# Seven row buffers instead of five, and a dense stage that gates each chunk at once with three activation tiles: one hybrid decoder layer on one Trainium2 core

## The chip, the cores and the metric

The kernel runs on one core of a Trainium2 chip. The metric is the device time of one execution in microseconds, the median of several runs; lower is better. Engines are named as the profile names them: PE (matrix engine), DVE (vector), ACT (scalar), POOL (GpSimd) and SP (the queue that issues most loads). The DMA engines move what SP, ACT and POOL issue.

## What is computed

One decoder layer for 1024 tokens of width 1024. An input projection feeds an mLSTM group of heads and an attention group of heads; both outputs are concatenated, projected and added to x. Then each token picks 128 single-neuron experts (8 heads, the best 16 of each) out of 16384, and adds what they give:

```python
def block(args):
    xb, ib, gb = args
    u = expert_u[ib]
    pre = jnp.einsum('td,tkd->tk', xb, u).astype(jnp.float32)
    a = jax.nn.gelu(pre, approximate=False) * gb
    return jnp.einsum('tk,tkd->td', a, expert_v[ib])
```

`ib` are a token's expert numbers and `gb` its gates (a softmax over the picked scores).

## The kernel before, in words

The 8 tiles of 128 tokens are cut into three groups: group 0 is tiles 0 and 1, group 1 tiles 2 to 5, group 2 tiles 6 and 7. Each group goes through a projection (`channels_in`, `project_*`), attention and mLSTM woven together (`attention`, `mlstm_half`), and `queries` (output projection, query projection, top-16 searches on DVE), then `pick`, which makes expert numbers and gates.

The experts are computed in two ways. Groups 0 and 2 are sparse: for each of a token's 128 experts, POOL gathers one row of 4 KB per token, 128 rows in one indirect DMA into a tile `gt` of 512 KB (`gather`, line 801), and DVE uses it in one instruction. `experts_in` (the U steps, line 813) multiplies and sums, `experts_out` (the V steps, line 854) multiplies and accumulates. For tile 0 the out step runs on PE instead (`experts_out_pe`, 64 steps with two gathers each, DVE line 835, PE line 842; called the W steps below). The order of the sparse work is fixed: U0 U1 W V1 U6 V6 U7 V7, where W is V0, with 128 gathers each.

Group 1 is dense. `spread_gates` writes a table of gates for all 16384 experts and its 512 tokens to DRAM (DVE line 722, ACT lines 726, 730 and 738, POOL line 732, 32 stores of 1 MB from line 739). `dense_experts` then runs over 16 expert groups of 8 chunks of 128 experts. A chunk's U part loads 512 KB (`ur`), splits it into a high and a low part on ACT and DVE (`uhi`, `ulo`), takes 24 matmuls of 512 columns into `pu`, and a Gelu on ACT (`da`, line 763). The gates of the expert group, 2 MB (`gg`, line 766), multiply `da` on DVE (line 769), the product is split (`dah`, `dal`), and the V part takes 24 matmuls a chunk into `pv`. That makes 6144 matmuls.

The program is written one part after another, but the order on each engine is made by a scheduler while the kernel is built. It moves an instruction past others as far as its inputs and the room in on-chip memory allow. Pools of tiles are stacked from two sides, and a pool opened where another lay must wait for the tiles there. The sparse pool that holds `gt` stays open from start to end, five tiles of 4 KB a partition; the pools of the dense stage are open only there. Each engine then runs its own list strictly in order.

Of the kernel before, what the change touches and what calls it, by code (L numbers as in the profile page):

```python
# [11 lines left out]
F32 = mybir.dt.float32  # L12
# [8 lines left out]
P = 128  # L21
T = 1024
D = 1024
# [7 lines left out]
EG = 8  # L31
TB = 16
# [11 lines left out]
def hybrid_layer(ctx, tc, x, g1, w_in, w_if, conv_w, conv_b, wq, wk, if_b, mh_g, skip, qn_g, kn_g,  # L44
                 rel_bias, onehot, w_out, g2, w_query, keys, expert_u, expert_ut, expert_v, out, dbg=None):
    nc = tc.nc
# [4 lines left out]
    sp = ctx.enter_context(tc.tile_pool(name="sparse", bufs=1))  # L51
# [12 lines left out]
    def pool(name, side="left"):  # L64
        return tc.tile_pool(name=name, bufs=1, side=side, reuse_waits="tile")
# [82 lines left out]
    def split(hi, lo, src):  # L148
        nc.scalar.copy(hi, src)
        nc.vector.tensor_tensor(lo, src, hi.bitcast(F32), op=ALU.subtract)  # L150

    def mm3(ps, lh, ll, rh, rl, first, last):
        nc.tensor.matmul(ps, lh, rh, start=first, stop=False)  # L153
        nc.tensor.matmul(ps, lh, rl, start=False, stop=False)  # L154
        nc.tensor.matmul(ps, ll, rh, start=False, stop=last)  # L155
# [552 lines left out]
    gate_d = dram.tile([GROUPS[DENSE][1] * P // TB, P, P * TB], F32, name="gate_d")  # L708
# [32 lines left out]
    def dense_experts(psu):  # L741

        tile0, TD = GROUPS[DENSE]
        DW = TD * P
        nb = DW // TB
        with pool("dh", "right") as dh, pool("du", "right") as du, pool("da", "right") as da, \
                pool("dl", "right") as dl, tc.tile_pool(name="psv", bufs=5, space=PS) as psv:
            th, tl = DENSE_IN
            acc = []
            for c0 in range(0, P, EG):  # L750
                ah, al, pre = [], [], []
                for c in range(c0, c0 + EG):
                    ur = du.tile([P, KD, P], F32, name="ur", bufs=2)
                    nc.sync.dma_start(ur, expert_ut[c])
                    uh = du.tile([P, KD, P], F32R, name="uhi", bufs=2)
                    nc.scalar.copy(uh, ur)  # L756
                    ul = du.tile([P, KD, P], F32R, name="ulo", bufs=2)
                    nc.vector.tensor_tensor(ul, ur, uh.bitcast(F32), op=ALU.subtract)  # L758
                    pp = psu.tile([P, DW], F32, name="pu")
                    for k in range(KD):  # L760
                        mm3(pp, uh[:, k], ul[:, k], th[:, k], tl[:, k], k == 0, k == KD - 1)
                    a = da.tile([P, DW], F32, name="da", bufs=EG + 1)
                    nc.scalar.activation(a, pp, AF.Gelu)  # L763
                    pre.append(a)
                gg = dl.tile([P, nb, EG, TB], F32, name="gg", bufs=1)
                nc.sync.dma_start(gg.rearrange("p b e t -> p b (e t)"),
                                  gate_d.rearrange("b p f -> p b f")[:, :, c0 * TB:(c0 + EG) * TB])
                for c, a in enumerate(pre, c0):
                    nc.vector.tensor_tensor(a.rearrange("p (b t) -> p b t", t=TB),
                                            a.rearrange("p (b t) -> p b t", t=TB), gg[:, :, c - c0], op=ALU.mult)  # L770
                    h = dh.tile([P, DW], F32R, name="dah", bufs=EG + 2)
                    l = dh.tile([P, DW], F32R, name="dal", bufs=EG + 2)
                    split(h, l, a)
                    ah.append(h)
                    al.append(l)
                if not acc:
                    for i in range(TD):
                        a = da.tile([P, D], F32, name="dacc", bufs=TD)
                        nc.sync.dma_start(a, x2_d[tile0 + i])
                        acc.append(a)  # L780
                for half in range(2):
                    cols = slice(half * 512, (half + 1) * 512)
                    po = [psv.tile([P, 512], F32, name="pv") for _ in range(TD)]
                    for c in range(c0, c0 + EG):
                        vr = dh.tile([P, 512], F32, name="vr", bufs=4)
                        nc.sync.dma_start(vr, expert_v.rearrange("(a c) d -> c a d", c=P)[c, :, cols])
                        vh = dh.tile([P, 512], F32R, name="vhi", bufs=2)
                        nc.scalar.copy(vh, vr)  # L788
                        vl = dh.tile([P, 512], F32R, name="vlo", bufs=2)
                        nc.vector.tensor_tensor(vl, vr, vh.bitcast(F32), op=ALU.subtract)  # L790
                        for i in range(TD):
                            s = slice(i * P, (i + 1) * P)
                            mm3(po[i], ah[c - c0][:, s], al[c - c0][:, s], vh, vl, c == c0, c == c0 + EG - 1)
                    for i in range(TD):
                        nc.vector.tensor_tensor(acc[i][:, cols], acc[i][:, cols], po[i], op=ALU.add)
            for i in range(TD):
                nc.sync.dma_start(out[(tile0 + i) * P:(tile0 + i + 1) * P], acc[i])

    def gather(table, idx, j):
        gt = sp.tile([P, D], F32, name="gt", bufs=5)  # L800
        nc.gpsimd.indirect_dma_start(out=gt, out_offset=None, in_=table,  # L801
                                     in_offset=bass.IndirectOffsetOnAxis(ap=idx[:, j:j + 1], axis=0))
        return gt
# [3 lines left out]
    def experts_in(t):  # L807
        h2 = sp.tile([P, D], F32, name="h2s", bufs=1)
        nc.sync.dma_start(h2, h2_d[t])
        pr = sp.tile([P, P], F32, name="pr_s", bufs=2)  # L810
        for j in range(P):
            gt = gather(expert_u, IDX[t], j)
            nc.vector.scalar_tensor_tensor(gt, gt, 1.0, h2, op0=ALU.mult, op1=ALU.mult,  # L813
                                           accum_out=pr[:, j:j + 1])
        a = sp.tile([P, P], F32, name="act", bufs=2)
        nc.scalar.activation(a, pr, AF.Gelu)
        nc.vector.tensor_tensor(a, a, GATE[t].rearrange("p h k -> p (h k)"), op=ALU.mult)
        COEF[t] = a
# [30 lines left out]
    def experts_out(t):  # L849
        acc = sp.tile([P, D], F32, name="acc", tag="acc", bufs=1)  # L850
        nc.sync.dma_start(acc, x2_d[t])
        for j in range(P):
            gt = gather(expert_v, IDX[t], j)
            nc.vector.scalar_tensor_tensor(acc, gt, COEF[t][:, j:j + 1], acc, op0=ALU.mult, op1=ALU.add)  # L854
        nc.sync.dma_start(out[t * P:(t + 1) * P], acc)
# [80 lines left out]
    for c in (psgx, pstx, psmx):  # L936
        c.__exit__(None, None, None)
    dense_experts(psu)
    psux.__exit__(None, None, None)
    ql.close()  # L940
    for step in "U0 U1 V0 V1 U6 V6 U7 V7".split():
        t = int(step[1])
# [81 lines left out]
```

## Time and profile before

| what | us |
|---|---|
| median of 3 runs (lowest, highest) | 3164.97 (3154.72, 3176.85) |
| the profiled execution's own time | 3162.73 |
| its span, from the first to the last instruction | 3160.9 |
| PE busy | 2763.9 |
| DVE busy | 2513.1 |
| POOL busy | 1439.0 |
| ACT busy | 1223.1 |

Times in views count from the span's start. The share of 16 DMA engines, the GB/s and the clock granted to PE are given by stretch; a clock of 1.0 is the upper of its two levels.

### The profile page before, as it was taken

What the parts mean: (1) busy time and instruction counts of PE and PEld (TensorE: products, weight loads), DVE (VectorE), ACT (ScalarE), POOL (GpSimd) and SP (SyncE); (2) the same over time, 40 slices, a digit from 0 to 9 for tenths busy, and PEclk for the clock granted to TensorE, in tenths of its full rate; (3) what the DMA queues carried; (4) which work ended last, traced back from release to release, by engine and by line L of the source; (5) the groups of instructions that cost most, each with busy time, mean ns of one, the idle gap of its engine ahead of it and who ended that gap; (6) DMA issues with size and microseconds to landing.
All of it is one profiled execution on the core that took longest, in us unless ns stands there. A gap on an engine that the chain in (4) does not pass through costs nothing.

```text
span 3160.9 us, 42101 instructions
## 1 busy us (share of the span) xinstructions
PE 2763.9 (87%) x13867; PEld 2180.5 (69%) x13867; DVE 2513.1 (80%) x5674; ACT 1223.1 (39%) x2265; POOL 1439.0 (46%) x1139
## 2 busy tenths in 40 slices
PE   6987766898679999776865999999999999999999
PEld 5877655676555554566753778787777888887787
DVE  4559986798854777899999888889887888988843
ACT  4643322454323223698972222233222332332222
POOL 0100665556643334465445555555554455555500
PEclk9979887797789999888986999999999999999999
DMA  6543899799987777688779999999999999999942
GB/s 195 180 157 112 300 312 359 277 321 325 318 278 253 247 263 258 192 298 297 261 241 329 346 325 336 335 331 329 324 326 325 319 339 344 326 326 340 321 144 74
DMA packets 370543, 891.45 MB, mean 282 GB/s; under 512 B 34023, under 2 KB 135399, under 8 KB 366228
## 3 DMA queue, kind: packets, MB, share of 16 engines
q0 software_dynamic: 147456, 536.94, 48.7%
q1 hardware_dynamic: 208724, 307.78, 29.4%
q10 hardware_dynamic: 14144, 44.05, 3.6%
q8 instruction: 109, 1.79, 0.2%
q14 instruction: 110, 0.90, 0.1%
HBM read 831.97 MB, written 61.38 MB: 283 GB/s over the span
## 4 chain that ended last, share of the span: by engine, by line
PE 38%; issue 17%; DVE 17%; DMA 15%; POOL 9%; ACT 3%; SPq 0%; POOLq 0%; DVEq 0%; ACTq 0%
POOL gt L801 9%; DMA gg<-gate_d 4%; PE accq L192 4%; DMA gt<-in_expert_u_dram,idx 4%; PE pu L154 3%; PE pv L154 3%; PE pu L155 3%; PE pu L153 3%; PE pv L155 3%; PE pv L153 3%; PE pov L842 3%; DVE gt L813 3%; DVE acc L854 2%; DMA gt<-in_expert_v_dram,idx 2%; PE acco L192 2%
## 5 line engine op out<-in xcount | busy, mean ns | idle before, releaser
L801 POOL DMA_INDIRECT gt<-in_expert_u_dram,idx x512 | 663.6, 1296 | 622.6 <-DVE gt L813 377.4
L801 POOL DMA_INDIRECT gt<-in_expert_v_dram,idx x384 | 502.3, 1308 | 432.5 <-DVE acc L854 320.0
L813 DVE SCALAR_TENSOR_TENSOR gt<-gt,h2s 128x1024 f32<-128x1024 f32 x512 | 617.5, 1218 | 64.3 <-DMA gt<-in_expert_u_dram,idx 63.3
L854 DVE SCALAR_TENSOR_TENSOR acc<-gt,act,acc 128x1024 f32<-128x1024 f32 x384 | 503.9, 1312 | 20.0 <-DMA gt<-in_expert_v_dram,idx 17.3
L153 PE MATMUL pu<-h2th,uhi 128*128 128x512 f32 x1024 | 409.4, 400 | 46.3 <-ACT da L763 27.9
L155 PE MATMUL pu<-h2th,ulo 128*128 128x512 f32 x1024 | 408.7, 399 | 10.8 <-DVE ulo L758 10.8
L154 PE MATMUL pv<-vlo,dah 128*128 128x512 f32 x1024 | 403.8, 394 | 9.6 <-DVE vlo L790 9.6
L154 PE MATMUL pu<-h2tl,uhi 128*128 128x512 f32 x1024 | 408.7, 399 | 0.0
L155 PE MATMUL pv<-vhi,dal 128*128 128x512 f32 x1024 | 401.6, 392 | 0.0
L788 ACT CAST vhi<-vr 128x512 fp32r<-128x512 f32 x256 | 157.4, 620 | 449.3 <-PE pv L155 428.0
L153 PE MATMUL pv<-vhi,dah 128*128 128x512 f32 x1024 | 319.6, 394 | 11.1 <-ACT vhi L788 7.4
L168 ACT CAST wh<-wr 128x512 fp32r<-128x512 f32 x291 | 178.5, 620 | 291.5 <-PE accq L192 64.5
L153 PEld LDWEIGHTS pu<-h2th,uhi 128*128 128x128 f32 x1024 | 194.9, 190 | 93.8 <-ACT da L763 29.1
L170 DVE TENSOR_TENSOR wl<-wr,wh 128x512 fp32r<-128x512 f32 x291 | 201.3, 700 | 71.6 <-ACT wh L168 70.5
L790 DVE TENSOR_TENSOR vlo<-vr,vhi 128x512 fp32r<-128x512 f32 x256 | 175.2, 685 | 92.2 <-ACT vhi L788 91.9
L756 ACT CAST uhi<-ur 128x1024 fp32r<-128x1024 f32 x128 | 134.4, 1051 | 271.8 <-PE pu L154 271.4
L801 POOL DMA_INDIRECT gt<-in_expert_v_dram,idxt x128 | 129.2, 1010 | 233.9 <-PE pov L842 204.3
L155 PEld LDWEIGHTS pu<-h2th,ulo 128*128 128x128 f32 x1024 | 194.5, 190 | 58.6 <-DVE ulo L758 12.2
L154 PEld LDWEIGHTS pv<-vlo,dah 128*128 128x128 f32 x1024 | 193.6, 189 | 56.9 <-DVE vlo L790 14.9
L153 PEld LDWEIGHTS pv<-vhi,dah 128*128 128x128 f32 x1024 | 192.4, 189 | 58.0 <-ACT vhi L788 11.3
L154 PEld LDWEIGHTS pu<-h2tl,uhi 128*128 128x128 f32 x1024 | 194.7, 190 | 46.3
L155 PEld LDWEIGHTS pv<-vhi,dal 128*128 128x128 f32 x1024 | 193.9, 189 | 41.9
(280 smaller groups left out, 5710.6 us busy)
## 6 DMA issues: line engine op xcount, KB each, us to landing
ur<-in_expert_ut_dram SPq DMA_DIRECT2D x128, 512.0 KB, 6.1
vr<-in_expert_v_dram SPq DMA_DIRECT2D x256, 256.0 KB, 5.6
wr<-in_w_in_dram SPq DMA_DIRECT2D x144, 256.0 KB, 4.8
gate_d<-gs ACTq DMA_DIRECT2D x32, 1024.0 KB, 6.7
gg<-gate_d SPq DMA_DIRECT2D x16, 2048.0 KB, 19.2
wr<-in_w_query_dram SPq DMA_DIRECT2D x96, 256.0 KB, 3.8
wr<-in_w_out_dram SPq DMA_DIRECT2D x48, 256.0 KB, 4.0
gt<-in_expert_u_dram,idx POOLq DMA_INDIRECT x512, 6.9
```

The lines of the kernel that those rows point to most:

```text
L153: nc.tensor.matmul(ps, lh, rh, start=first, stop=False)
L154: nc.tensor.matmul(ps, lh, rl, start=False, stop=False)
L155: nc.tensor.matmul(ps, ll, rh, start=False, stop=last)
L168: nc.scalar.copy(wh, wr)
L170: nc.vector.tensor_tensor(wl, wr, wh.bitcast(F32), op=ALU.subtract)
L192: nc.tensor.matmul(o, l, r, start=k == 0 and c == 0 and j == 0, stop=k == KD - 1 and j == 2, skip_group_check=True)
L756: nc.scalar.copy(uh, ur)
L788: nc.scalar.copy(vh, vr)
L790: nc.vector.tensor_tensor(vl, vr, vh.bitcast(F32), op=ALU.subtract)
L801: nc.gpsimd.indirect_dma_start(out=gt, out_offset=None, in_=table, in_offset=bass.IndirectOffsetOnAxis(ap=idx[:, j:j + 1], axis=0))
L813: nc.vector.scalar_tensor_tensor(gt, gt, 1.0, h2, op0=ALU.mult, op1=ALU.mult, accum_out=pr[:, j:j + 1])
L854: nc.vector.scalar_tensor_tensor(acc, gt, COEF[t][:, j:j + 1], acc, op0=ALU.mult, op1=ALU.add)
```

## The change

`gt` has seven buffers instead of five. In the dense stage the load of an expert group's gates stands ahead of the group's eight U parts instead of behind them; the gate product and its split follow each chunk's Gelu at once; and `da` has three buffers instead of nine (8 + 1). Nothing is computed differently. A `da` tile is 2 KB a partition, a `gt` tile 4 KB.

```diff
             for c0 in range(0, P, EG):
-                ah, al, pre = [], [], []
+                ah, al = [], []
+                gg = dl.tile([P, nb, EG, TB], F32, name="gg", bufs=1)
+                nc.sync.dma_start(gg.rearrange("p b e t -> p b (e t)"),
+                                  gate_d.rearrange("b p f -> p b f")[:, :, c0 * TB:(c0 + EG) * TB])
                 for c in range(c0, c0 + EG):
...
-                    a = da.tile([P, DW], F32, name="da", bufs=EG + 1)
+                    a = da.tile([P, DW], F32, name="da", bufs=3)
                     nc.scalar.activation(a, pp, AF.Gelu)
-                    pre.append(a)
-                gg = dl.tile([P, nb, EG, TB], F32, name="gg", bufs=1)
-                nc.sync.dma_start(gg.rearrange("p b e t -> p b (e t)"),
-                                  gate_d.rearrange("b p f -> p b f")[:, :, c0 * TB:(c0 + EG) * TB])
-                for c, a in enumerate(pre, c0):
                     nc.vector.tensor_tensor(a.rearrange("p (b t) -> p b t", t=TB),
                                             a.rearrange("p (b t) -> p b t", t=TB), gg[:, :, c - c0], op=ALU.mult)
...
-        gt = sp.tile([P, D], F32, name="gt", bufs=5)
+        gt = sp.tile([P, D], F32, name="gt", bufs=7)
```

The scheduler makes another order of it, well outside the lines of the diff. The lines of the changed kernel are up to three lower or higher than before (801 is 799, 813 is 811, 854 is 852, 769 is 767, 758 is 761, 790 is 788).

On POOL, before, in the second attention stretch: `idx` with expert_u are the U gathers, `rqo` is a step of a projection (here group 2's), `rmo` one of an mLSTM head (here group 1's).

```order
L161 TENSOR_TENSOR rqo<-rq,mhalf 128x8
L801 DMA gt<-in_expert_u_dram,idx 128x1024 x7
L161 TENSOR_TENSOR rqo<-rq,mhalf 128x8
L801 DMA gt<-in_expert_u_dram,idx 128x1024
L161 TENSOR_TENSOR rmo<-rm,mhalf 128x2
L801 DMA gt<-in_expert_u_dram,idx 128x1024 x6
L161 TENSOR_TENSOR rqo<-rq,mhalf 128x8
L801 DMA gt<-in_expert_u_dram,idx 128x1024 x12
L161 TENSOR_TENSOR rmo<-rm,mhalf 128x2
```

The same engine now, from the last mLSTM heads of group 1 on; `idxt` are the W gathers.

```order
L161 TENSOR_TENSOR rmo<-rm,mhalf 128x2
L799 DMA gt<-in_expert_u_dram,idx 128x1024 x18
L799 DMA gt<-in_expert_v_dram,idxt 128x1024 x4
L161 TENSOR_TENSOR rmo<-rm,mhalf 128x2
L799 DMA gt<-in_expert_v_dram,idxt 128x1024 x9
L161 TENSOR_TENSOR rso<-rs,mhalf 128x1
L799 DMA gt<-in_expert_v_dram,idxt 128x1024 x8
L161 TENSOR_TENSOR rso<-rs,mhalf 128x1
L799 DMA gt<-in_expert_v_dram,idxt 128x1024 x56
L161 TENSOR_TENSOR rqo<-rq,mhalf 128x8
L799 DMA gt<-in_expert_v_dram,idxt 128x1024 x8
L161 TENSOR_TENSOR rqo<-rq,mhalf 128x8
```

The projection of group 2 (`rso`, `rqo`) has moved behind the whole attention and mLSTM of group 1, to the W gathers.

On POOL, before, from the W gathers to the first gates; `rmo` is now mLSTM of group 2, `expert_v` with `idx` the V gathers of tile 1, `e` a step of `spread_gates`.

```order
L801 DMA gt<-in_expert_v_dram,idxt 128x1024 x6
L161 TENSOR_TENSOR rmo<-rm,mhalf 128x2
L801 DMA gt<-in_expert_v_dram,idxt 128x1024 x40
L161 TENSOR_TENSOR rmo<-rm,mhalf 128x2
L801 DMA gt<-in_expert_v_dram,idxt 128x1024 x52
L161 TENSOR_TENSOR rmo<-rm,mhalf 128x2
L801 DMA gt<-in_expert_v_dram,idxt 128x1024 x7
L801 DMA gt<-in_expert_v_dram,idx 128x1024 x9
L161 TENSOR_TENSOR rmo<-rm,mhalf 128x2
L801 DMA gt<-in_expert_v_dram,idx 128x1024 x5
L732 TENSOR_TENSOR e_11013<-hot,grow 128x512
```

The same place now; `r2o` is a step of `queries` of group 1.

```order
L799 DMA gt<-in_expert_v_dram,idxt 128x1024 x27
L799 DMA gt<-in_expert_v_dram,idx 128x1024 x12
L161 TENSOR_TENSOR r2o<-r_8430,mhalf 128x4
L799 DMA gt<-in_expert_v_dram,idx 128x1024 x116
L161 TENSOR_TENSOR rmo<-rm,mhalf 128x2 x4
L732 TENSOR_TENSOR e_11013<-hot,grow 128x512
```

All 128 V gathers of tile 1, and behind them the attention and mLSTM of group 2, now stand ahead of the first gates. On DVE, where before 9 of these V steps were ahead of the first gate instruction and 78 ahead of the last, all 128 are ahead of the first now.

On DVE, now, at the end of `spread_gates` (`hot`) and the start of the dense stage:

```order
L722 TENSOR_TENSOR hot<-ids,key_107 128x512 x5
L811 SCALAR_TENSOR_TENSOR gt,pr_s<-gt,h2s 128x1024 x6
L761 TENSOR_TENSOR ulo<-ur,uhi 128x1024
L811 SCALAR_TENSOR_TENSOR gt,pr_s<-gt,h2s 128x1024
L761 TENSOR_TENSOR ulo<-ur,uhi 128x1024
L811 SCALAR_TENSOR_TENSOR gt,pr_s<-gt,h2s 128x1024 x6
L761 TENSOR_TENSOR ulo<-ur,uhi 128x1024
L811 SCALAR_TENSOR_TENSOR gt,pr_s<-gt,h2s 128x1024 x7
L767 TENSOR_TENSOR da<-da,gg 128x512 x3
```

Before, the first two gate products stood behind both picks of group 2, and three U parts of each later expert group were split ahead of its first gate product; that number is three now as well. On PE 96 matmuls of U parts stand ahead of the last matmul of `spread_gates` now, and none before.

## Rows read from the trace of the kernel before

**Rows 1.** Busy time of each engine, clock, DMA in six stretches of the span.

```profile
core 0: us, PE busy (x) PEld busy (x) DVE busy (x) ACT busy (x) POOL busy (x), PEclk, DMA share, GB/s
505.00:895.00 390.00, 290.05 (x1563) 226.61 (x1563) 317.07 (x746) 149.37 (x328) 223.92 (x182) 0.77 0.91 318
895.00:1310.00 415.00, 401.67 (x1979) 223.14 (x1979) 267.65 (x1308) 128.00 (x258) 152.28 (x149) 0.97 0.74 247
1310.00:1637.00 327.00, 244.22 (x1671) 225.26 (x1670) 318.00 (x795) 299.91 (x608) 171.44 (x136) 0.89 0.78 270
1637.00:1730.00 93.00, 33.15 (x104) 24.40 (x105) 86.27 (x169) 19.09 (x22) 54.29 (x41) 0.61 0.90 311
1730.00:3010.00 1280.00, 1263.02 (x5416) 1020.49 (x5416) 1095.22 (x1456) 376.46 (x568) 691.73 (x515) 0.99 0.94 330
3010.00:3154.00 144.00, 143.84 (x627) 117.27 (x625) 55.87 (x78) 40.19 (x61) 0.00 (x0) 1.00 0.31 93
```

**Rows 2.** One line each: ns min/median/max, first and last start in us.

```profile
L835 DVE SCALAR_TENSOR_TENSOR wv<-iota,aT x64: 202/225/227, 894.8 to 1252.4; 128x64 f32<-128x64 f32 x64
...
L722 DVE TENSOR_TENSOR hot<-ids,key x256: 396/411/1929, 1310.5 to 1630.3; 128x512 bf16<-128x512 bf16 x128
...
L738 ACT COPY gs<-pg x128: 988/1059/1162, 1318.4 to 1636.1; 128x512 f32<-128x512 f32 x128
```

**Rows 3.** PE's waits by the instruction that waits, 1637 to 1730 us.

```profile
PE pu L153 <- ACT da L763: 27.9, 2, 27.1
PE pu L153 <- ACT uhi L756: 18.4, 1, 18.4
PE pu L155 <- DVE ulo L758: 10.8, 2, 7.5
PE pv L153 <- ACT dah L149: 3.7, 1, 3.7
```

**Rows 4.** Groups of DVE instructions by line, 505 to 895 us.

```profile
L813 DVE SCALAR_TENSOR_TENSOR gt<-gt,h2s 128x1024 f32<-128x1024 f32 x167 | 202.4, 1219 | 26.7 <-DMA gt<-in_expert_u_dram,idx 26.4
L170 DVE TENSOR_TENSOR wl<-wr,wh 128x512 fp32r<-128x512 f32 x55 | 37.2, 686 | 5.1 <-ACT wh L168 5.1
```

**Rows 5.** DMA issues: KB each, median us from issue to landing.

```profile
wr<-in_w_in_dram SPq DMA_DIRECT2D x144, 256.0 KB, 4.8
gate_d<-gs ACTq DMA_DIRECT2D x32, 1024.0 KB, 6.7
gg<-gate_d SPq DMA_DIRECT2D x16, 2048.0 KB, 19.2
gt<-in_expert_u_dram,idx POOLq DMA_INDIRECT x512, 6.9
```

**Rows 6.** The page's GB/s in 40 slices of 79 us.

```profile
GB/s 195 180 157 112 300 312 359 277 321 325 318 278 253 247 263 258 192 298 297 261 241 329 346 325 336 335 331 329 324 326 325 319 339 344 326 326 340 321 144 74
```

**Rows 7.** PE in order of time: start, us, instruction.

```profile
647.01 0.28 PE L192 MATMUL accz<-htl,wh 128*128 128x256 f32 x1
647.13 0.28 PE L192 MATMUL accz<-hth,wl 128*128 128x256 f32 x1
...
1089.16 1.06 PE L842 MATMUL pov<-gt,wv 128*32 128x512 f32 x6
1090.15 0.50 PE L192 MATMUL accq<-h2tl,wh 128*128 128x512 f32 x1
...
1091.04 1.05 PE L842 MATMUL pov<-gt,wv 128*32 128x512 f32 x2
1092.02 0.50 PE L192 MATMUL accq<-h2tl,wh 128*128 128x512 f32 x1
```

**Rows 8.** DVE instructions on gathered tiles alone, 895 to 1310 us.

```profile
895.00:1310.00 415.00, 18.60 (x21) 0.97 0.74 247
```

**Rows 9.** The page's costliest groups: the V steps.

```profile
L854 DVE SCALAR_TENSOR_TENSOR acc<-gt,act,acc 128x1024 f32<-128x1024 f32 x384 | 503.9, 1312 | 20.0 <-DMA gt<-in_expert_v_dram,idx 17.3
```

**Rows 10.** DVE's waits, 1637 to 3161 us: the gate product.

```profile
DVE da L769 <- DMA gg<-gate_d: 89.9, 14, 8.2
```

## The prediction

> **What bounds the kernel now.** I read busy time by stretch first, because the shares over the whole span mix stages with different limits [rows 1]. Call the six stretches A (505 to 895 us), B (to 1310), C (to 1637), D (from there to the end at 3160.9, three rows). The cut at 505 is mine, shortly before the attention of group 1; moving it changes both sums alike. The other cuts are events: the W steps run from 894.8 to 1252.4, the first gate instruction of `spread_gates` is at 1310.5, and its last copy out of PSUM starts at 1636.1 [rows 2].
>
> The reader is to see a different limit in each. In A the DMA engines are the limit: share 0.91 at 318 GB/s, while DVE has 317 of 390 us. In B it is PE, 402 of 415, since the W steps stand woven between the matmuls of `queries` and attention; DVE has only 268 and DMA 0.74. In C it is DVE, 318 of 327, with ACT at 300 right behind. In D it is PE: 5416 matmuls in 1280 us are 0.236 us each, and once the gathers have ended 627 in 144 us are 0.230, so the gathers cost the dense matmuls almost nothing [rows 1]. PE's idle time in D lies at its start, 27.9 + 18.4 + 10.8 + 3.7 = 61 us [rows 3]. So the end of the kernel is the time at which the dense stage can run freely, plus a fixed dense stage, and the question is when that time comes.
>
> **The change part by part.** No instruction is added or removed. Two things change: how far POOL may run ahead (seven tiles instead of five), and the order that the scheduler makes. The order weighs most. `gt` lies in a pool that is open throughout, so two more tiles take 8 KB a partition from every stage, while the smaller `da` gives 12 KB back in the dense stage alone. I take that to be why what shared memory before now runs one after another; the order itself, whatever its reason, shows that it does. The projection of group 2 leaves stage A and goes to the W steps. `queries` of group 1 comes behind the W steps, its picks behind that, then the attention of group 2, all with the 128 V gathers of tile 1, and only then the gates.
>
> Stage A now, without that projection. DMA before: 318 GB/s times 390 us are 124 MB [rows 1]. The projection loads 49 blocks of 256 KB [rows 5], 13 MB, and by the code reads and writes about 4 MB more. That leaves 107 MB, at about 325 GB/s 330 us. DVE gives up 49 x 0.686 = 34 us of splits [rows 4] and by my estimate 17 for the convolution and the rest, and keeps 266. I take 330; it ends at 835. Bounds: 298 (107 MB at 359 GB/s, the best slice of the page [rows 6]) and 390, as before.
>
> Stage B1, new: 64 W steps with the projection of group 2. DMA has 128 x 0.524 + 17 = 84 MB [rows 5], at 330 GB/s 255 us. PE has two bursts of 1.0 us a step (1089.16 to 1090.15, 1091.04 to 1092.02), 128 us, and 576 projection matmuls at 0.12 us, 69 us, together 197 [rows 7]. I take 255. Bounds: 200, PE alone, and 357, the pace of the W steps before [rows 2].
>
> Stage B2, new: `queries` and picks of group 1, attention of group 2 and the V steps. DVE in B had 268 us [rows 1]; take off the W steps, 64 x 0.225 = 14 [rows 2], and 19 of gather steps [rows 8]; add about 8 for the part of the picks that stood behind the first gates before, and 128 V steps of 1.312, 168 us [rows 9]. The sum is 411 us. DVE was 0.81 busy in A and 0.97 in C; nearer to C, at 0.92, this takes 450. Bounds: 424 (0.97) and 510 (0.81).
>
> A rule speaks against the change here, and the order shows how. Before, a stage bound by PE (the W steps) and one bound by DVE (`queries`) lay on each other; now they lie behind each other, and DVE, which needs 14 + 34 + 17 = 65 of the 255 us in B1, idles through most of it. The Trainium skill, "Perfetto Trace Analysis", section "Optimization Strategy", says that a kernel whose most-contended engine changes over time may gain by interleaving those regimes. By that rule the change, which takes regimes apart, loses; by the bare sum of DVE work in B1 and B2, 476 us, B1 would cost next to nothing beyond it. Rows 1 agree with the rule: B alone was full on PE while DVE was free.
>
> Stage C now has no V steps between the gates, but ACT was at 300 of 327 us, and the order gives it about 14 more (copies of the picks, splits and Gelus of the dense start). So the relief of DVE is worth little here. I keep 327; bounds 313 (ACT's 300 + 14 without a gap) and 340.
>
> Stage D before: 1637 to 3160.9 is 1524 us. Of the 61 us of idle time at its start [rows 3] two waits were for ACT, whose Gelus stood behind the picks; the picks stand inside C now. From the last gate copy the chain is the store (6.7), `gg` (19.2) [rows 5], and about 2 for product and split: 28 us. PE works 6 of them on a fifth U part, so 22 are idle; and 96 matmuls at 0.236, 23 us, are done inside C. Ten more for the ramp: 1524 - 61 + 22 - 23 + 10 = 1472. Bounds 1456 and 1524.
>
> In the steady dense loop I cost the edits at nothing. The earlier `gg` and the three `da` hide behind the fact that three U parts stood ahead of a group's first gate product before, and three do now. DVE already waited 6.4 us for `gg` at 14 of 16 groups [rows 10] without PE waiting for it. If that cover goes, the price is in the rivals. The seven buffers themselves I cost at nothing where DMA is full; they help the W steps, which is in the 255 us.
>
> The sum is 505 + 330 + 255 + 450 + 327 + 1472 = 3339 us of span. The profiled execution took 1.8 us more than its span, and the median is 2.2 us above that execution: 3343 us, 5.6% slower.
>
> **The rivals.** First, not slower: with seven tiles the gathers land ahead of every use, and each stage runs at its busiest compute engine's sum. Then A is 266 (DVE), B1 197 (PE), B2 411 (DVE), C 313 (ACT), D 1462: 505 + 266 + 197 + 411 + 313 + 1462 + 4 = 3158 us, no change. For it: DVE was 0.97 busy in C with five buffers. Against it: A would need 107 MB in 266 us, 402 GB/s, and the best slice is 359 [rows 6]. It decides if the first gate instruction comes before about 1390 us. Faster than that needs stages to lie on each other again, which the order on DVE forbids.
>
> Second, more bandwidth: two more gathers in flight lift the DMA rate to the 359 GB/s of the best slice. A becomes 298 and B1 234, 53 us less: 3290. Against it: at a share of 0.91 to 0.94 the rate was 318 to 330 [rows 1]. The Trainium skill, "HBM Reference", section "Specifications (TRN2)", puts a core that streams alone at about 425 GB/s; by that figure A would be at DVE's 266 and B1 at PE's 197, and the estimate by the page is 3221. No row here comes near its rate.
>
> Third, the W steps keep their pace of 5.6 us, because a gather's issue, landing (6.9 us [rows 5]) and use limit them and not PE: B1 is 357 and the time 3445. For it: DMA was only 0.74 busy in B; against it, PE was full there.
>
> Fourth, with three `da` the wait for `gg` reaches PE: 15 groups x 6.4 us = 96 us, 3439.
>
> **How the numbers follow.** Forecast 0.62, not slower 0.07, bandwidth 0.13, W pace 0.12, `gg` 0.06. The forecast's own terms reach down by 32, 55, 26, 14 and 16 and up by 60, 102, 60, 13 and 52; as independent errors they make about 70 down and 145 up. With the rivals at 3290 and 3445 the range is 3245 to 3450, and leaves out the case of no change and the far ends. A measurement of this kernel can tell about 1% from no change. Slower by over 1%, above 3197, is the forecast and three rivals less a little: 0.91. Within 1% 0.06, faster 0.03.
>
> **What would show it.** Right: the projection of group 2 beside the W steps and behind all scores of group 1; the last W step near 1090, the first gate instruction near 1540, the last gate copy near 1867; DVE well under half busy during the W steps; the U steps of tile 6 near the end of the gates, not 45 V steps there; dense matmuls still at 0.23 to 0.24 us. Wrong: a first gate instruction before 1400, which would mean that I overrate what is lost by taking the stages apart; or new waits of PE on Gelus or gate products at each expert group.

## The result, and the profile after

The changed kernel takes 3436.45 us (median of 4 runs, 3429.69 to 3459.03), the kernel before 3168.24 us on the same chip: a ratio of 1.0863, 95% interval [1.0799, 1.0927]. The forecast was 3343 us and 5.6% slower, with a range of 3245 to 3450. The direction holds and the time lies inside the range, 14 us below its upper end; the size was too small by 93 us.

The profiled execution took 3438.11 us, its span is 3436.3 us. Busy time of each engine, clock and DMA of the changed kernel by stretch; the cuts are the events named below, and each row answers to one of [rows 1]:

```profile
core 0: us, PE busy (x) PEld busy (x) DVE busy (x) ACT busy (x) POOL busy (x), PEclk, DMA share, GB/s
0.00:398.00 398.00, 294.01 (x1803) 256.74 (x1804) 221.71 (x846) 160.39 (x341) 22.43 (x29) 0.82 0.45 135
398.00:572.00 174.00, 112.90 (x643) 97.46 (x642) 157.59 (x290) 47.61 (x76) 138.24 (x97) 0.81 0.95 345
572.00:893.00 321.00, 233.79 (x950) 161.73 (x949) 267.14 (x637) 93.09 (x226) 220.40 (x177) 0.65 0.91 325
893.00:1125.00 232.00, 204.06 (x1225) 108.26 (x1226) 71.65 (x183) 60.60 (x107) 140.76 (x126) 0.99 0.98 356
...
1125.00:1510.00 385.00, 182.18 (x880) 138.32 (x878) 352.16 (x1202) 78.21 (x139) 174.66 (x132) 0.71 0.69 226
1510.00:1650.00 140.00, 129.84 (x559) 84.97 (x558) 46.13 (x161) 52.39 (x118) 2.80 (x4) 0.73 0.24 76
1650.00:1989.00 339.00, 262.58 (x1769) 237.99 (x1768) 288.51 (x891) 312.06 (x621) 124.37 (x105) 0.90 0.61 219
...
1989.00:2060.00 71.00, 40.24 (x160) 32.05 (x161) 55.37 (x90) 14.70 (x23) 42.65 (x30) 0.76 0.92 324
2060.00:3160.00 1100.00, 1092.77 (x4721) 885.24 (x4720) 946.46 (x1230) 327.31 (x495) 598.06 (x443) 1.00 0.95 333
3160.00:3429.00 269.00, 268.67 (x1168) 218.96 (x1166) 109.06 (x149) 77.82 (x117) 0.00 (x0) 1.00 0.34 103
```

The W steps and the first and last gate instructions, which the cuts come from, by line in the changed kernel (as [rows 2]; line 833 was 835):

```profile
L833 DVE SCALAR_TENSOR_TENSOR wv<-iota,aT x64: 188/225/227, 893.3 to 1124.7; 128x64 f32<-128x64 f32 x64
...
L722 DVE TENSOR_TENSOR hot<-ids,key x256: 395/414/1924, 1651.0 to 1973.6; 128x512 bf16<-128x512 bf16 x128
...
L738 ACT COPY gs<-pg x128: 989/1154/1498, 1656.5 to 1987.7; 128x512 f32<-128x512 f32 x128
```

The reader is to see three things. Ahead of the gates the limits now lie one behind another: from 893 DMA is full (share 0.98), with PE at 204 of 232 us and DVE at 72; from 1125 DVE is (352 of 385), and PE has 182; from 1510 PE is (130 of 140, at a granted clock of 0.73 of its upper level), DVE has 46, and DMA is nearly idle at a share of 0.24. Before the change, PE's full stretch and the queries on DVE were one stretch of 415 us. The first gate instruction comes at 1651 instead of 1310, 340 us later; the last gate copy at 1988 instead of 1636. And the dense stage then runs faster than before: 1100 us for 4721 matmuls is 0.233 us each, against 0.236 [rows 1].

By the stages of the prediction, in us (start is up to the attention of group 1, cut 174 us behind the first U step in both):

| stage | before | predicted | measured after |
|---|---|---|---|
| start | 505 | 505 | 572 |
| A, attention of group 1 | 390 | 330 | 321 |
| B1, W steps and projection of group 2 | B: 415 | 255 | 232 |
| B2, queries, picks, V steps, attention of group 2 | in B | 450 | 525 |
| C, gates | 327 | 327 | 338 |
| D, last gate copy to the end | 1524 | 1472 | 1448 |

The errors are +67, -9, -23, +75, +11 and -24: +97 us of span in all (3436 against 3339).

PE's waits at the dense start of the changed kernel, 1930 to 2060 us (as [rows 3]: engine, line waited for, total us, times, longest):

```profile
PE pv L153 <- ACT dah L149: 30.7, 1, 30.7
PE pg L737 <- issue: 5.6, 2, 3.0
PE pu L155 <- DVE ulo L761: 3.8, 3, 3.0
```

One wait is left, 31 us from 1994 on, at the first V part, which waits for the first gate product. That is the chain of store and `gg` that the prediction laid behind the last gate copy.

### The profile page after: what moved, and what is told of

Same layout as the page of the kernel before. It is cut to its first block, busy times and chain, and to the rows that moved or that the text cites. A ratio compares the mean times of both kernels' runs of the same rounds, so it can differ in the third digit from the quotient of the medians.

```text
span 3436.3 us, 42247 instructions
## 1 busy us (share of the span) xinstructions
PE 2821.0 (82%) x13867; PEld 2221.7 (65%) x13867; DVE 2516.6 (73%) x5673; ACT 1224.2 (36%) x2259; POOL 1464.4 (43%) x1139
## 4 chain that ended last, share of the span: by engine, by line
PE 53%; DVE 20%; DMA 11%; issue 9%; ACT 4%; POOL 3%; SPq 1%; DVEq 0%; ACTq 0%; POOLq 0%
PE pu L155 6%; PE pu L154 6%; PE pu L153 6%; PE pv L153 6%; PE pv L154 6%; PE pv L155 6%; DVE gt L811 3%; DMA gg<-gate_d 3%; PE sc L509 3%; POOL gt L799 3%; PE po L530 2%; PE acco L192 2%; DVE wl L170 2%; DVE acc L852 2%; DVE hot L722 2%
## 5 line engine op out<-in xcount | busy, mean ns | idle before, releaser
L799 POOL DMA_INDIRECT gt<-in_expert_u_dram,idx x512 | 675.7, 1320 | 514.0 <-DVE gt L811 257.4
L799 POOL DMA_INDIRECT gt<-in_expert_v_dram,idx x384 | 519.4, 1353 | 474.9 <-DVE acc L852 266.5
L852 DVE SCALAR_TENSOR_TENSOR acc<-gt,act,acc 128x1024 f32<-128x1024 f32 x384 | 491.0, 1279 | 3.5 <-DMA acc<-x 0.3
L170 DVE TENSOR_TENSOR wl<-wr,wh 128x512 fp32r<-128x512 f32 x291 | 197.9, 687 | 92.6 <-ACT wh L168 90.8
L153 PEld LDWEIGHTS pv<-vhi,dah 128*128 128x128 f32 x1024 | 192.6, 189 | 82.7 <-ACT dah L149 31.1
L737 PE MATMUL pg<-e,e 128*128 128x128 f32 x1024 | 160.1, 311 | 64.3 <-ACT gs L738 47.1
L761 DVE TENSOR_TENSOR ulo<-ur,uhi 128x1024 fp32r<-128x1024 f32 x128 | 156.3, 1222 | 63.0 <-ACT uhi L759 59.8
```

Source lines behind the costliest of these rows:

```text
L170: nc.vector.tensor_tensor(wl, wr, wh.bitcast(F32), op=ALU.subtract)
L737: nc.tensor.matmul(pg[:, j], e1[:, j0 + j], e2[:, j0 + j], start=True, stop=True)
```

## The experiments

Theory at the outset: two more `gt` tiles take room, the scheduler then lays stages apart, and that costs the time, while the dense edits and the buffers themselves are worth next to nothing. The rivals: the dense edits cost it, or the further run-ahead of the gathers does.

**The dense edits alone**, with the five buffers and the order of before:

```diff
-        gt = sp.tile([P, D], F32, name="gt", bufs=7)
+        gt = sp.tile([P, D], F32, name="gt", bufs=5)
```

> The dense stage's edits alone, with five gt tiles. Theory R (room: what costs is that two more gt tiles take 8 KB a partition from every stage, and stages that lay beside each other run one after another): the order up to the gates is that of the kernel before, so 3168 us within 1%; the start waits of the dense stage (61 us of PE idle) stay, since the Gelus still stand behind the picks. Rival D (the dense edits cost the time, three da and the early gg): 3300 to 3440 us. Rival T (the gathers' run-ahead costs it): 3168 us too.

Measured: 3166.2 us (10 runs), ratio to before 0.9992 [0.9962, 1.0021]. The first gate instruction comes at 1303, the last copy at 1626. The edits cost nothing and give nothing. That rival falls.

**Room alone**: the kernel of the run above, so five buffers, with one tile beside them that nothing reads, of 512, 1024 or 2048 columns: 2, 4 or 8 KB a partition. 8 KB is what the two buffers take.

```diff
     sp = ctx.enter_context(tc.tile_pool(name="sparse", bufs=1))
+    room = sp.tile([P, 512], F32, name="room", bufs=1)
+    nc.vector.memset(room, 0.0)
```

With 2 KB the attention of group 2 moves behind the queries and picks of group 1, and 110 V steps stand ahead of the first gate; with 4 KB the projection of group 2 moves behind the attention of group 1 as well; with 8 KB also the mLSTM and attention of group 0 behind its own projection, and the order of the stages is that of the changed kernel.

> Dense edits, five gt tiles, and an unused tile of 2 KB a partition in the same pool. Its order puts the attention of group 2 behind queries and picks of group 1, as the changed kernel does; the projection of group 2 stays beside the attention of group 1. Theory R: slower than the dense edits alone by 60 to 120 us, since attention of group 2 alone took 128 us of scores in the changed kernel with DVE a third busy, and part of that comes back at the start of the dense stage. Rival T: no change, 3168 us.

> As before with 4 KB. Now the projection of group 2 also stands behind the attention of group 1, beside the W steps. Theory R: another 30 to 100 us on top of the run with 2 KB. Rival T: 3168 us.

> As before with 8 KB, the room that two gt tiles take, with five gt tiles. Its order is that of the changed kernel up to small shifts: mLSTM and attention of group 0 stand behind its projection as well. Theory R: another 50 to 80 us on top of the run with 4 KB (the first U step came 68 us later in the changed kernel), and in all 3440 to 3520 us: the changed kernel's 3436 plus what two more buffers give back. Rival T: 3168 us, far below the changed kernel.

Measured: 3278.13 us, 1.0349 [1.0302, 1.0396]; 3406.75 us, 1.0759 [1.0708, 1.081]; 3430.98 us, 1.0811 [1.0758, 1.0864]. Against the run of the dense edits alone that is +112, a further +129 and a further +24 us. The first step is as expected, the second larger, the third smaller (its total is also 9 us below the expected range); between the last two the intervals overlap. What counts: a tile that nothing reads makes the kernel as slow as the change does (1.0811 against 1.0863, overlapping intervals). The run-ahead of the gathers is no cause, since these kernels have five buffers.

Where the time is lost, by events in the profiled executions (us from the span's start):

| | before | 2 KB | 4 KB | 8 KB | changed |
|---|---|---|---|---|---|
| first U step | 330 | 363 | 354 | 390 | 398 |
| first W step | 895 | 923 | 844 | 882 | 893 |
| last W step | 1252 | 1234 | 1195 | 1232 | 1125 |
| first score of group 2's attention (DVE line 511) | 920 | 1292 | 1456 | 1494 | 1514 |
| first gate instruction | 1310 | 1489 | 1587 | 1653 | 1651 |
| last gate copy | 1636 | 1821 | 1921 | 1985 | 1988 |
| end of the span | 3161 | 3275 | 3375 | 3440 | 3436 |

The whole loss is there at the first gate instruction; behind it some 65 us come back (from there to the end it is 1851 us before and 1785 to 1788 in the four others). The event that moves most is the attention of group 2: it began at 920, on top of the W steps, and begins at 1292 to 1514 behind the queries. The row of the first U step explains the start. With 2 KB, the 32 input transposes of group 1 (`pt`, PE line 203), which stood in fours between the matmuls of group 0's attention and ended at 186 us, stand behind that attention and end at 218; in the changed kernel, where the mLSTM of group 0 (163 to 211) begins behind the projection as well, they end at 253.

**One more buffer in the same order.** Six buffers keep the stages in the order of the 4 KB run.

```diff
-        gt = sp.tile([P, D], F32, name="gt", bufs=7)
+        gt = sp.tile([P, D], F32, name="gt", bufs=6)
```

> Six row buffers with the dense edits. The order on every engine keeps the stages as in the run with a 4 KB tile and five buffers (3406.75 us), so this run prices one more buffer in the same order. Theory (the order costs the time, a buffer gives next to nothing): 3385 to 3430 us. Rival (the buffers are worth what the W steps show, 350 us with five against 232 us with seven, so some 60 us for one more): about 3350 us.

Measured: 3424.29 us, 1.0843 [1.0788, 1.0899], as the theory has it; no gain. Yet the W steps did become faster. The run with 4 KB and five buffers, by stretch (W steps; queries and V steps; attention of group 2):

```profile
844.00:1195.00 351.00, 309.07 (x1738) 184.57 (x1737) 153.79 (x491) 95.04 (x184) 160.87 (x146) 0.93 0.85 291
1195.00:1445.00 250.00, 80.75 (x365) 57.94 (x363) 239.61 (x890) 44.46 (x63) 120.71 (x93) 0.65 0.69 219
1445.00:1587.00 142.00, 122.86 (x562) 79.60 (x562) 97.94 (x208) 51.89 (x118) 52.94 (x45) 0.79 0.70 240
```

The run with six buffers, the same three:

```profile
845.00:1156.00 311.00, 264.49 (x1570) 154.81 (x1569) 121.21 (x271) 83.13 (x164) 170.41 (x149) 0.94 0.91 325
1156.00:1469.00 313.00, 126.54 (x534) 90.86 (x533) 291.39 (x1129) 57.02 (x84) 140.72 (x108) 0.68 0.67 210
1469.00:1635.00 166.00, 144.64 (x562) 95.12 (x562) 82.41 (x193) 52.13 (x118) 34.12 (x28) 0.65 0.47 159
```

The sixth buffer takes 40 us off the W stretch (351 to 311), and the next one is 63 us longer (250 to 313): fewer of the query matmuls lie beside the W steps (PE 265 of busy time instead of 309), and more follow. Only the projection and queries lead to the gates; the W steps do not. In the changed kernel the DMA side of this shows. The gathers (queue q0) and the loads of group 2's projection in it, 893 to 1115 us:

```profile
DMA packets 27725, 78.44 MB, mean 353 GB/s; under 512 B 3043, under 2 KB 6115, under 8 KB 27710
...
q0 software_dynamic: 16600, 60.45, 74.1%
...
wr<-in_w_in_dram SPq DMA_DIRECT2D x42, 256.0 KB
...
gt<-in_expert_v_dram,idxt POOLq DMA_INDIRECT x115
```

The same loads in the run with 8 KB and five buffers, 882 to 1071 us:

```profile
DMA packets 22529, 60.13 MB, mean 318 GB/s; under 512 B 2438, under 2 KB 5510, under 8 KB 22515
...
q0 software_dynamic: 11691, 42.56, 63.7%
...
wr<-in_w_in_dram SPq DMA_DIRECT2D x42, 256.0 KB
...
gt<-in_expert_v_dram,idxt POOLq DMA_INDIRECT x66
```

The same 42 weight loads and what hangs on them take 222 us with seven buffers and 189 with five, though the rate is higher. The gathers take 60 MB of the traffic instead of 43, which I take to be the cause; no run isolates it.

**Seven buffers in the dense stage alone.** Five throughout; two more lie in a pool opened ahead of the U steps of tile 6, where the smaller `da` has left room. The order ahead of it is that of before.

```diff
+    late = Scope("late", "right")
...
+        taken[0] += 1
+        if LATE and taken[0] % 7 in (2, 5):
+            gt = LATE[0].tile([P, D], F32, name="gtl", bufs=2)
+        else:
+            gt = sp.tile([P, D], F32, name="gt", bufs=5)
```

> Five row buffers throughout and two more that exist only in the dense stage, where the smaller da has left room; the order ahead of the dense stage is that of the kernel before. Theory (in the dense stage PE is the limit and the gathers are hidden with five buffers already): within 0.5% of the kernel before, 3155 to 3185 us by this chip's runs. Rival (the two more buffers do help the dense stage): dense matmuls at the 0.230 us that they take without gathers instead of 0.236 us, about 30 us faster, 3140 us.

Measured: 3182.01 us (12 runs), 1.0058 [1.0036, 1.0079]: inside the theory's range in us, just outside its 0.5%, so a little slower than before rather than equal. In the trace two effects stand against each other. The dense stretch of this run, which answers to the fifth of [rows 1], and PE's waits from 1625 to 1735 us:

```profile
1730.00:3010.00 1280.00, 1270.19 (x5482) 1029.20 (x5481) 1086.76 (x1443) 385.69 (x577) 668.54 (x501) 1.00 0.93 325
```

```profile
PE pu L153 <- ACT uhi L759: 92.6, 1, 92.6
PE pu L155 <- DVE ulo L761: 8.8, 1, 8.8
```

5482 matmuls instead of 5416 in 1280 us are 0.2335 us each instead of 0.2363: over 6144 matmuls, 17 us less. So the rival had a part of the truth. But PE stands 92.6 us at the first U part, where before its waits were 61 us in all [rows 3]. On ACT's list copies of the picks of group 2 (line 668), which wait for DVE, and the load of the first `ur` lie ahead of that split:

```profile
L668 ACT COPY of<-ixf 128x2048 bf16<-128x2048 bf16 x4 | 7.6, 1898 | 42.1 <-DVE one L672 32.2 <-DVE ixf L658 9.9
...
L759 ACT CAST uhi<-ur 128x1024 fp32r<-128x1024 f32 x3 | 3.1, 1045 | 31.1 <-DMA ur<-in_expert_ut_dram 31.1
```

The last figures are ACT's idle time ahead of each, 1600 to 1735 us: 42.1 for the picks and 31.1 for the load. Before, four of these splits (1653 to 1672 us) stood ahead of three of the four copies; here the first split, at 1706, is behind all four. The traced execution is the fastest of the twelve, though, with a span 2.6 us shorter than the traced one before: its gates end 22 us earlier (1614), and the dense stage behind them takes 1544 us instead of 1525. So the trace shows the two effects, but the 0.6% between the medians is not accounted for by it.

**Four buffers**, so 4 KB more room than before:

```diff
-        gt = sp.tile([P, D], F32, name="gt", bufs=7)
+        gt = sp.tile([P, D], F32, name="gt", bufs=4)
```

> Four row buffers with the dense edits, so 4 KB a partition more room than before. The order on DVE has the V steps of tile 1 all behind the gates and the W steps a little more spread. Theory (the order of before was already free of the room, and one buffer less slows the stages that wait for gathers): the W steps go from 357 us to at most 446 us, so 3170 to 3270 us, likeliest 3220. Rival (room is worth time beyond what before has): faster than before, 3100 to 3150 us.

Measured: 3197.42 us, 1.0115 [1.0071, 1.0159]; the total is in the theory's range, but not by its path. The W steps take 485 us (893 to 1378), more than the bound of 446, and it does no harm: the gates start at 1288 while W steps still run, and the last copy is at 1626. What is lost is lost in the dense stage (1573 us from the last copy to the end, 1525 before). Its costliest groups on DVE in the page:

```profile
L811 DVE SCALAR_TENSOR_TENSOR gt<-gt,h2s 128x1024 f32<-128x1024 f32 x512 | 620.9, 1220 | 136.7 <-DMA gt<-in_expert_u_dram,idx 134.4
L852 DVE SCALAR_TENSOR_TENSOR acc<-gt,act,acc 128x1024 f32<-128x1024 f32 x384 | 496.2, 1292 | 97.2 <-DMA gt<-in_expert_v_dram,idx 94.2
```

The same groups in the changed kernel:

```profile
L811 DVE SCALAR_TENSOR_TENSOR gt<-gt,h2s 128x1024 f32<-128x1024 f32 x512 | 619.7, 1228 | 29.6 <-DMA gt<-in_expert_u_dram,idx 28.6
L852 DVE SCALAR_TENSOR_TENSOR acc<-gt,act,acc 128x1024 f32<-128x1024 f32 x384 | 491.0, 1279 | 3.5 <-DMA acc<-x 0.3
```

DVE waits 229 us for gathers with four tiles and 29 with seven (the last figure of each row, but for the last row, whose wait is for `x`). With four, the last V step is at 3193, behind the last dense matmul at 3158, so the gathers set the end; before, V ended at 3010, 151 us ahead of the end, and DVE waited 17 us for V gathers [rows 9]. Not all of that is the buffer's: in this order 35 V steps stand ahead of the last gate copy instead of 80, so 45 more, 58 us of DVE work, fall into the dense stage. DVE's wait for gathers is 81 us with five tiles before, and 93 with five and the idle 8 KB. So the fifth buffer has a large part in that cover, and the sixth and seventh widen it.

**Room given back elsewhere.** The changed kernel with two instead of three tiles each for the weights on their way (6 KB); the kernel with five buffers and the same; and with five buffers and one input tile `xt` instead of two (4 KB; a one-row tile that shares its buffers goes from two to one with it):

```diff
-        wr = wts.tile([P, 512], F32, name="wr", bufs=3)
+        wr = wts.tile([P, 512], F32, name="wr", bufs=2)
...
-                xt = xp.tile([P, D], F32, name="xt", tag="xt", bufs=2)
+                xt = xp.tile([P, D], F32, name="xt", tag="xt", bufs=1)
```

> The changed kernel with two instead of three of each of the three tiles that a weight chunk passes through, which gives 6 KB back. The order then has the mLSTM of group 0 beside its projection again and the projection of group 2 beside the attention of group 1; the V steps of tile 1 stay ahead of the gates. Theory (the order costs the time): the 67 us of the start come back and some 40 of what followed, 3330 us, range 3290 to 3380. Rival (two weight tiles starve the projections, 49 chunks a group with each step waiting for the load): no gain, 3420 us or more.

> Five row buffers with the dense edits and two instead of three of each of the three tiles that a weight chunk passes through, which gives 6 KB back. The order has 21 V steps ahead of the first gate instead of 9. Theory: the two weight tiles cost the projections 10 to 40 us and the room returns little, 3165 to 3210 us. Rival (two are enough, and room is worth time): below 3150 us.

> Five row buffers with the dense edits and one input tile xt instead of two, which gives 4 KB a partition back: as much room as the run with four row buffers had, with the buffers of before. Theory (that run lost its time only in the stages that wait for gathers, and its order is the better one): the first gate no later than 1288 us, the dense stage as before, 3120 to 3160 us. Rival (the order of before was free of the room already, and one xt tile makes each transpose wait for its load): 3165 us or more.

Measured: 3351.9 us, 1.0603 [1.0557, 1.0648]; 3251.09 us, 1.0256 [1.023, 1.0283]; 3178.65 us, 1.0033 [1.0013, 1.0054]. With two weight tiles the seven-buffer kernel gains 85 us and the five-buffer kernel, which had its overlaps already, loses 85 (more than expected). There the first U step, the first W step and the first gate come 23, 45 and 69 us later than before, so the stages up to the gates all lose some; slower projections would fit that, but the cause was not isolated. So giving room back pays where stages were apart and costs elsewhere. The 67 us of the start come back only in part (first U step 379 instead of 398). One `xt` tile loses a little, and its first gate, at 1313, is not the earlier one that was expected: the rival holds there. Its first U step is at 360 instead of 330, and PE's transposes wait 27 us for `xt` ahead of it, where before none of these waits is in the trace. No version was faster than before.

**The V steps ahead of the picks.** In the changed kernel from 1400 to 1510 us DVE is busy for 108 of 110 us and PE for 6. First that stretch, then the DVE group of the V steps in it:

```profile
1400.00:1510.00 110.00, 6.38 (x14) 2.38 (x14) 107.91 (x167) 16.37 (x18) 83.36 (x52) 0.50 0.80 264
```

```profile
L852 DVE SCALAR_TENSOR_TENSOR acc<-gt,act,acc 128x1024 f32<-128x1024 f32 x58 | 74.0, 1277 | 0.1
```

The experiment shrinks them, on tile 1 alone:

```diff
-            nc.vector.scalar_tensor_tensor(acc, gt, COEF[t][:, j:j + 1], acc, op0=ALU.mult, op1=ALU.add)
+            w = 64 if t == 1 else D
+            nc.vector.scalar_tensor_tensor(acc[:, :w], gt[:, :w], COEF[t][:, j:j + 1], acc[:, :w],
+                                           op0=ALU.mult, op1=ALU.add)
```

> The changed kernel, with the V steps of tile 1 on DVE cut to 64 of 1024 columns (the other columns of tile 1's output are left without these terms); the gathers and the order of the stages stay. In the changed kernel DVE is 352 of 385 us busy between the last W step and the first matmul of the attention of group 2 (1125 to 1510), 58 V steps take 74 us in the last 110 of them, and PE idles there. Theory (the V steps stand in DVE's queue ahead of the picks that the attention of group 2 waits for, so DVE sets this stretch): some 150 us of DVE work go, the gathers and weights then need about 230 us for 80 MB, and 85 to 135 us come back: 3300 to 3350 us. Rival (the chain of queries and picks sets it, and the V steps only fill DVE's gaps): less than 30 us, 3405 us or more. Either way the attention of group 2 alone stays at about 140 us.

Measured: 3355.53 us, 1.0594 [1.0551, 1.0636], 81 us less than the changed kernel. By stretch (W steps; queries and V steps; attention of group 2):

```profile
893.00:1127.00 234.00, 205.68 (x1226) 108.79 (x1225) 71.72 (x181) 60.80 (x107) 140.25 (x125) 0.98 0.97 353
1127.00:1422.00 295.00, 173.58 (x882) 135.31 (x880) 226.10 (x1193) 77.32 (x139) 135.30 (x129) 0.77 0.82 279
1422.00:1554.00 132.00, 113.73 (x560) 75.47 (x560) 47.78 (x170) 52.16 (x119) 6.45 (x8) 0.82 0.36 118
```

The middle stretch falls from 385 to 295 us, and the first gate comes at 1554 instead of 1651. So the V steps stood on the path: the picks wait in DVE's queue behind them, and the attention of group 2 behind the picks. The saving of 81 us is 4 short of the expected range; 226 us of DVE work are left where about 200 were reckoned, and nothing is full any more in that stretch. (The traced execution is the fastest of its four.) The attention alone still takes 132 us, with DVE at 48 and PE at 114 of them; what sets it is PE, as the next section shows.

## Why the prediction was right and where it fell short

**Room makes the order: right, and now shown.** The prediction took it from the order that two tiles of `gt` push stages apart. A tile of 8 KB that nothing reads does the same, to within the intervals.

**Edits of the dense stage at nothing: right** (0.9992).

**The 505 at the head of the sum was the first failed step: 572.** The sum began with the attention of group 1 and carried everything ahead of it over ("moving it changes both sums alike"), though there too the order had changed: the mLSTM and attention of group 0 stand behind its projection, and the transposes of group 1 behind both. That is 67 us, the first U step at 398 instead of 330. The cut after is set at the same distance from the first U step, so start and A are best read together: 893 instead of 835.

**B2 "the sum is 411 us ... at 0.92, this takes 450" was the second: 525.** The stage is two. Up to 1510 DVE is busy 352 of 385 us, 0.91, so the rule of the step holds there almost to the figure. Behind it stands the attention of group 2, with 46 us of DVE work, and takes 140. The step left PE out: B before had 402 us of PE [rows 1], the W steps take 128 of them by the prediction's own count, and the 274 that are left are in no term of B2. That would do no harm if they lay under DVE's work, as some of them do up to 1510; but the attention stands behind the picks, and its PE work lies under nothing. From 1510 to 1650 PE is busy for 130 of 140 us, and these are all its waits:

```profile
PE sc L509 <- DMA wqk<-in_wk_dram: 4.1, 1, 4.1
PE sc L509 <- DMA kp<-kT: 3.2, 2, 1.7
PE po L530 <- ACT pb L528: 2.5, 5, 0.8
PE po L530 <- DMA vp<-va: 0.2, 1, 0.2
```

DVE and ACT wait for PE's scores (`sc`) and transposes (`pp`), or for each other's results on them, in the same stretch:

```profile
DVE ss L511 <- PE sc L509: 52.2, 25, 5.4
ACT ss L515 <- DVE mx L514: 31.9, 13, 11.5
ACT pb L528 <- PE pp L526: 29.6, 23, 3.9
```

Followed back from 1650, the chain of what released what lies on PE for 114 of the 140 us. The clock has a part in it. The first 56 us of the stretch and the 34 behind them, and two score matmuls (start, us) from either side of the rise:

```profile
1510.00:1566.00 56.00, 51.77 (x146) 31.21 (x145) 14.78 (x51) 13.67 (x30) 0.71 (x1) 0.50 0.29 95
1566.00:1600.00 34.00, 31.80 (x181) 21.85 (x179) 13.80 (x47) 17.67 (x41) 0.70 (x1) 0.98 0.36 108
```

```profile
1562.68 2.07 PE L509 MATMUL sc<-kp,qp 64*128 64x512 f32 x2
1567.82 1.12 PE L509 MATMUL sc<-kp,qp 64*128 64x512 f32 x2
```

PE's busy time times its granted clock gives an estimate of what the attention would take at the upper level: 130 x 0.73 = 95 us here, 114 x 0.82 = 93 with the small V steps, 148 x 0.65 = 96 with the idle 8 KB (1494 to 1653) and 123 x 0.79 = 97 with 4 KB. In all four the stretch is PE's busy time and 10 to 19 us more. Before, the same matmuls lay from 920 to 1290 between the W steps, at a clock of 0.97 [rows 1]. 46 us at 0.92 are 50, so the term was 90 us short there, and 15 too high in the rest.

**A (321 for 330), C (338 for 327): right.** In A DMA is at 0.91 and 325 GB/s, as the step assumed. In C ACT has 312 us of 339.

**B1 255, measured 232: the mechanism was right, the rate too low.** The W steps ran at the DMA limit, but at 356 GB/s instead of 330: 84 MB by 356 are 236 us. The second rival (more bandwidth) was right in this stage, and the third (W pace) wrong with seven buffers; with five in the same order the W steps did take 350 us. But the W steps do not lead to the gates. With seven buffers the projection beside them is later by 33 us, and the first gate comes at 1651 as against 1653 with five and the idle tile. That fits with a total that seven buffers in place of an idle tile do not change by anything that can be measured; it is read from one trace of each.

**D 1472, measured 1448: off by 24 us.** "In the steady dense loop I cost the edits at nothing" holds for the edits. What changed is the matmul: 0.2330 us instead of 0.2363, over 6144 matmuls 20 us. Only a part of that is the buffers'. With five buffers and the idle 8 KB, in the same order of stages, the dense stretch is

```profile
2030.00:3190.00 1160.00, 1146.05 (x4936) 927.99 (x4935) 994.46 (x1306) 345.15 (x517) 619.04 (x471) 1.00 0.94 331
```

or 0.2350 us a matmul, and D is 1455. So the two buffers give some 7 us of the 24. The rest came with the order, which has 48 more V steps and some 24 more U steps done by the last gate copy than before. In orders nearer to that of before, four buffers take 0.2450 (5224 in 1280 us), five 0.2363, the two late ones 0.2335; each is one traced execution.

**The other side.** The rival without loss (first gate ahead of 1390) is refuted by the first gate at 1651. DVE still waits for `gg` (93 us at 14 groups, 90 before [rows 10]), but PE's waits from 2060 on are 7 us in all, none of them for a Gelu or a gate product, so that rival falls too. The regime rule that the prediction cited from the Trainium skill, "Perfetto Trace Analysis", section "Optimization Strategy", agrees: PE-bound and DVE-bound work, 415 us when interleaved, takes 757 here, with the V steps of tile 1 and the projection of group 2 in it.

**Inside the range, in part by luck.** The two failed steps together are 142 us short. The start had no bound of its own, and B2's 525 lies above its bound of 510. The total stayed 14 us inside the range because A, B1 and D came out 56 us shorter than forecast.

**What stays open.** How the loss divides between 4 and 8 KB: profiled executions and medians differ by up to 30 us there. Why two weight tiles cost the five-buffer kernel 85 us. Seven buffers from the start with the whole order of before were not tried, so the value of seven buffers ahead of the dense stage, with all stages overlapping, is not known.

## What to carry to other kernels

A buffer count is also a room count: before two more tiles are priced as run-ahead, look in the new order at which stages no longer lie beside each other, from the very first instruction on. Price a stage that now stands alone by the engine that is fullest in it, at the clock granted there, and do not add its work to another engine's sum. And a faster transfer stream that does not lead to the next gate can take its bandwidth from the one that does.

## What the runs showed of the hardware

With seven tiles, so up to seven indirect gathers of 512 KB in flight, the core moved 356 GB/s over 232 us at a DMA share of 0.98; with five, in the same order, 318 GB/s at 0.91 over the loads of the projection (189 us). The Trainium skill, "HBM Reference", section "Specifications (TRN2)", gives about 425 GB/s for a core that streams alone; no run here came near it over such a stretch.

The granted clock of PE (1.0 is 2.4 GHz, 0.5 is 1.2) was lower in stretches where a stage stood alone: 0.65 in the attention of group 1 (0.77 while a projection lay beside it [rows 1]) and 0.71 and 0.73 in the two stretches ahead of the gates. What went before the last shows in the rows above: PE was busy for 6 of the 110 us up to 1510, at 0.50; it stayed at 0.50 for 56 us, though busy for 52 of them, and was at 0.98 for the 34 behind. So PE's work takes longer just where no other work hides it: 560 matmuls of group 2's attention were busy for 130 us at 0.73 and for 114 at 0.82.
